# Other TensorE durations in a planned instruction order: a hybrid decoder trunk in float32 on one core

## The chip, the cores and the metric

The kernel runs on one core of a Trainium2 chip. The metric is device time in microseconds (us). Five engines work side by side, each through its own list of instructions, in order: TensorE (PE, with its weight loads as PEld), VectorE (DVE), ScalarE (ACT), GpSimd (POOL) and SyncE (SP), which issues the transfers from memory. The program's order is fixed when it is built; at run time each engine only waits for the semaphores of what it needs.

## The reference, cut to what matters

A trunk of two layers over one sequence of 256 positions of width 1024. Each layer is a feed-forward block (half weight), a token mixer, and a second feed-forward block; every block is normalised and modulated by vectors made of a conditioning vector `c`.

```python
def modulate(x, g, shift, scale):
    return rmsnorm(x, g) * (1.0 + scale[:, None, :]) + shift[:, None, :]

def swiglu(h, w_gu, w_down):                  # w_gu 1024 x 5632, w_down 2816 x 1024
    g, u = jnp.split(h @ w_gu, 2, axis=-1)
    return (jax.nn.silu(g) * u) @ w_down

c_act = jax.nn.silu(c)
for l in range(2):
    mod = (c_act @ w_mod[l] + b_mod[l]).reshape(1, 9, 1024)      # w_mod[l] 1024 x 9216
    h = modulate(x, g_norm[l, 0], mod[:, 0], mod[:, 1])
    x = x + 0.5 * mod[:, 2][:, None, :] * swiglu(h, w_ffn1_gu[l], w_ffn1_down[l])
    h = modulate(x, g_norm[l, 1], mod[:, 3], mod[:, 4])
    x = x + mod[:, 5][:, None, :] * hybrid_mixer(h, ...)         # w_in 1024 x 2048, w_out 1024 x 1024
    h = modulate(x, g_norm[l, 2], mod[:, 6], mod[:, 7])
    x = x + 0.5 * mod[:, 8][:, None, :] * swiglu(h, w_ffn2_gu[l], w_ffn2_down[l])
return rmsnorm(x, g_final)
```

The mixer projects `h` once, runs windowed attention, a gated linear recurrence and a short convolution on parts of the result, and sends all three through one output projection.

## The kernel before

**Products.** Float32 accuracy comes from splitting each operand into a high and a low part. A weight block of 1024 rows and 128 columns is loaded (`raw`), ACT casts its high part (`wH`, line 336) and DVE subtracts to get the low part (`wL`, line 341). The activations are split in the same way into `zH` (line 413) and `zL` (line 416). A product then takes three matmuls of 256 or 258 columns (`mm3`, lines 348 to 350: high by high, high by low, low by high), in the down projection two, one of 256 and one of 512 columns (`mm2`, lines 355 and 356).

**Stages.** Each feed-forward block has 22 output pairs of gate and up columns (`pair`, 8 steps of two products), an evacuation (line 473), a gated activation into `hp`, and then 8 output columns of the down projection with 22 products each, whose sums are added to the residual `xT` (line 491). In the last block before a new stage the next `zH` and `zL` are made right behind each such addition. The mixer does its projections as pairs, its elementwise parts on DVE and ACT, and 64 products of the output projection. The very first block is special (`first`): the modulation of its first eight 128-wide slices is computed on PE (line 975), reduced on DVE (line 979), folded on PE (line 984), turned into scale and shift (lines 987 to 989), and applied (lines 998 to 1003) slice pair by slice pair, while 12 products per slice run in k order.

**Modulation.** The other 16 vectors of `mod` are computed on DVE: each takes 8 transfers of 512 KB (`mraw`, line 368) and 8 passes (lines 373 and 375), one reduction (line 379), a small product on PE and an addition (line 387). One such transfer with its pass is called a *piece* below. They depend on nothing but `c`, so they can stand anywhere before their use; only three `mraw` buffers exist.

**What sets the order.** Every step is put into a list with an engine, an assumed duration, and what it reads and writes (`add`). `due` walks this list backwards and gives each step a latest start, counted from where PE would be if its assumed durations simply followed each other. `emit` then plays the list forward: at each moment it takes the engine that can start earliest, and on it the step with the earliest latest start among those that can start within 0.06 us. Buffers are limited (three `raw`, three `mraw`, eight pairs of `wH` and `wL`, three PSUM tiles for products). The steps are written out in the order of these planned starts. So the assumed durations decide which step an engine's list has first; at run time they have no effect of their own.

The assumed durations of PE's products are the constants `C3` and `C3U` at line 358: `2 * C3U` for a step of a pair (line 482), `2 * C3` for two products of the first block (line 537), `C3` for a product of the down projection (line 568) and of the mixer's output projection (line 844).

## Time and profile before

| | us |
|---|---|
| median of 3 runs | 978.92 |
| lowest and highest | 978.75 and 979.3 |
| the profiled execution, device time | 978.36 |
| its span, first to last instruction | 976.6 |
| PE busy in the span | 957.1 |
| DVE busy | 798.2 |
| ACT busy | 503.1 |
| mean TensorE clock granted, share of full speed | 0.996 |

The profiled execution took 978.36 us, 0.56 us under the median, and its span is 1.76 us shorter than its device time. The views used further down are the page's busy times, busy times by stretches of the span, the waits of an engine summed by what it waited for, and the instructions of one engine in order of time. A square bracket at a row's end gives the idle time of the engine just before it and what ended it. Matmuls overlap, so the pitch from one start to the next, not the printed length, is what a matmul costs PE.

### The profile page before, as it was taken

The numbers are of one execution on the slowest core, as the hardware profiler recorded it, in microseconds if no ns is written. First come the engines' busy times: TensorE is split into PE (matmuls) and PEld (weight loads), VectorE is DVE, ScalarE is ACT, GpSimd is POOL, SyncE is SP. The second block draws the span as 40 slices with busy tenths as digits, with TensorE's granted clock in tenths as the row PEclk, the third lists the DMA queues.
The fourth block names the chain that finished last, engine by engine and source line by source line (L and its number), as shares of the span: only waits on it lengthen the run. The fifth ranks groups of instructions, "written<-read, shape, count | busy, mean of one in ns | idle before, by whom it ended". The sixth has DMA issues, their size and how long they took to land.

```text
span 976.6 us, 18186 instructions
## 1 busy us (share of the span) xinstructions
PE 957.1 (98%) x7407; PEld 905.9 (93%) x7407; DVE 798.2 (82%) x1195; ACT 503.1 (52%) x780; POOL 21.7 (2%) x24
## 2 busy tenths in 40 slices
PE   7999999999999999999999999999999999999997
PEld 6889999889998999998899999988998999999886
DVE  5588989999989999989789976687999998766651
ACT  3446645454865554444454544444577555544431
POOL 5000000000000000000000000000000000000000
PEclk9999999999999999999999999999999999999998
DMA  9976889998946989997878965598785776756421
GB/s 331 367 243 222 272 283 301 364 307 292 246 161 228 301 275 327 311 308 253 294 230 295 312 199 184 190 311 264 253 232 173 249 251 212 243 179 194 163 76 44
DMA packets 185784, 242.76 MB, mean 249 GB/s; under 512 B 6504, under 2 KB 164452, under 8 KB 185700
## 3 DMA queue, kind: packets, MB, share of 16 engines
q1 hardware_dynamic: 185160, 240.96, 75.5%
q8 instruction: 58, 0.95, 0.4%
q10 hardware_dynamic: 540, 0.63, 0.2%
q14 instruction: 26, 0.21, 0.1%
HBM read 240.52 MB, written 1.05 MB: 247 GB/s over the span
## 4 chain that ended last, share of the span: by engine, by line
PE 91%; DVE 3%; DMA 3%; issue 1%; ACT 1%; ACTq 0%; POOLq 0%; DVEq 0%; SPq 0%
PE gu L348 22%; PE gu L349 22%; PE gu L350 22%; PE gu L356 15%; PE gu L355 8%; DMA hp_t<-in_w_mod_dram 1%; DVE wL L341 1%; DMA mraw_t<-in_w_mod_dram 1%; DMA sq_t<-in_b_mod_dram 1%; DVE xT L491 1%; PE gu L632 1%; PE gu L693 1%; DVE macc_t L375 1%; PE s L712 0%; PE s L752 0%
## 5 line engine op out<-in xcount | busy, mean ns | idle before, releaser
L348 PE MATMUL gu<-zH,wH 128*128 128x258 f32 (+1 forms) x1664 | 472.5, 284 | 2.5 <-ACT zH L1002 2.5
L349 PE MATMUL gu<-zL,wH 128*128 128x258 f32 (+1 forms) x1664 | 469.8, 282 | 1.1 <-DVE zL L416 0.3
L350 PE MATMUL gu<-zH,wL 128*128 128x258 f32 (+1 forms) x1664 | 470.7, 283 | 0.0
L336 ACT CAST wH<-raw_t 128x1024 fp32r<-128x1024 f32 (+1 forms) x324 | 320.2, 1015 | 283.8 <-PE gu L356 116.3
L341 DVE TENSOR_TENSOR wL<-raw_t,wH 128x1024 fp32r<-128x1024 f32 (+1 forms) x324 | 375.7, 1181 | 62.8 <-ACT wH L336 61.4
L348 PEld LDWEIGHTS gu<-zH,wH 128*128 128x128 f32 x1664 | 315.3, 189 | 4.8 <-ACT zH L1002 3.9
L349 PEld LDWEIGHTS gu<-zL,wH 128*128 128x128 f32 x1664 | 315.5, 190 | 3.1 <-DVE zL L416 1.9
L350 PEld LDWEIGHTS gu<-zH,wL 128*128 128x128 f32 x1664 | 314.4, 189 | 0.0
L356 PE MATMUL gu<-hp_t,wH 128*128 128x512 f32 x704 | 247.9, 393 | 0.0
L355 PE MATMUL gu<-hp_t,wL 128*128 128x256 f32 x704 | 200.4, 285 | 1.2 <-DVE xT L491 1.2
L356 PEld LDWEIGHTS gu<-hp_t,wH 128*128 128x128 f32 x704 | 132.2, 188 | 29.6
L375 DVE SCALAR_TENSOR_TENSOR macc_t<-mraw_t,cact,macc_t 128x1024 f32<-128x1024 f32 x112 | 143.4, 1280 | 5.6 <-DMA mraw_t<-in_w_mod_dram 5.5
L355 PEld LDWEIGHTS gu<-hp_t,wL 128*128 128x128 f32 x704 | 132.3, 188 | 1.9 <-PE gu L1100 1.1
L473 DVE TENSOR_TENSOR ev_t<-gu,Rb 128x514 f32<-128x514 f32 x98 | 67.5, 690 | 47.4 <-PE gu L350 46.8
L517 ACT CAST hp_t<-h_t 128x256 fp32r<-128x256 f32 x88 | 35.6, 404 | 75.1 <-DVE h_t L515 74.9
L513 ACT ACTIVATE sg_t<-ev_t 128x256 f32<-128x256 f32 x88 | 44.1, 502 | 38.7 <-DVE ev_t L473 35.9
L491 DVE SCALAR_TENSOR_TENSOR xT<-gu,gv_t,xT 128x256 f32<-128x256 f32 x80 | 36.7, 479 | 16.7 <-PE gu L356 16.0
L518 DVE TENSOR_TENSOR hp_t<-h_t,hp_t 128x256 fp32r<-128x256 f32 x88 | 36.9, 420 | 9.0 <-ACT hp_t L517 8.8
L515 DVE SCALAR_TENSOR_TENSOR h_t<-ev_t,sg_t 128x256 f32<-128x256 f32 x88 | 41.7, 475 | 0.5 <-ACT sg_t L513 0.2
L349 PE MATMUL gu<-hp_t,wH 128*128 128x256 f32 x128 | 36.2, 283 | 1.8 <-DVE hp_t L832 1.8
L348 PE MATMUL gu<-hp_t,wH 128*128 128x256 f32 x128 | 37.2, 290 | 0.0
L350 PE MATMUL gu<-hp_t,wL 128*128 128x256 f32 x128 | 36.1, 282 | 0.0
(167 smaller groups left out, 498.2 us busy)
## 6 DMA issues: line engine op xcount, KB each, us to landing
raw_t<-in_w_ffn_gu_dram SPq DMA_DIRECT2D x82, 1024.0 KB, 6.8
mraw_t<-in_w_mod_dram SPq DMA_DIRECT2D x128, 512.0 KB, 6.8
raw_t<-in_w_ffn_down_dram SPq DMA_DIRECT2D x32, 1024.0 KB, 5.4
raw_t<-in_w_ffn_down_dram SPq DMA_DIRECT2D x16, 768.0 KB, 6.7
raw_t<-in_w_in_dram SPq DMA_DIRECT2D x12, 1024.0 KB, 6.4
hp_t<-in_w_mod_dram SPq DMA_DIRECT2D x8, 1024.0 KB, 11.2
raw_t<-in_w_ffn_gu_dram SPq DMA_DIRECT2D x16, 384.0 KB, 8.2
raw_t<-in_w_in_dram SPq DMA_DIRECT2D x8, 512.0 KB, 5.0
```

The costliest lines, as they stand in the source:

```text
L336: A.copy(dst(0), view(raw()))
L341: V.tensor_tensor(out=dst(1), in0=view(raw()), in1=h, op=ALU.subtract)
L348: PE.matmul(ps, lhsT=wh[:, wi, :], rhs=aH, start=first, stop=False, skip_group_check=True)
L349: PE.matmul(ps, lhsT=wh[:, wi, :], rhs=aL, start=False, stop=False, skip_group_check=True)
L350: PE.matmul(ps, lhsT=wl[:, wi, :], rhs=aH, start=False, stop=last, skip_group_check=True)
L355: PE.matmul(ps[:, 0:S], lhsT=wl[:, wi, :], rhs=a[:, 0, :], start=first, stop=False, skip_group_check=True)
L356: PE.matmul(ps, lhsT=wh[:, wi, :], rhs=a, start=False, stop=last, skip_group_check=True)
L375: V.scalar_tensor_tensor(out=acc(), in0=raw(), scalar=cact[:, k:k + 1], in1=acc(), op0=ALU.mult, op1=ALU.add)
L473: V.tensor_tensor(out=t()[:, :, 0:257], in0=ps()[:, :, 0:257], in1=Rb[:, R, 0:257].unsqueeze(1).to_broadcast([128, 2, 257]), op=ALU.mult)
L491: add("DVE", 0.4, lambda: V.scalar_tensor_tensor(out=xT[:, d, :], in0=src(), scalar=gv()[:, d:d + 1], in1=xT[:, d, :], op0=ALU.mult, op1=A ...
L513: add("ACT", ca(S, 1), lambda: A.activation(out=sg(), in_=t()[:, 0, 0:S], func=ACTF.Silu, bias=bg_()), r=[t], w=[sg])
L515: add("DVE", 0.4, lambda: V.scalar_tensor_tensor(out=h(), in0=t()[:, 1, 0:S], scalar=bu_(), in1=sg(), op0=ALU.add, op1=ALU.mult), r=[t, sg ...
```

## The change

One more constant, and three other values: a product in three matmuls of 256 columns is now assumed at 0.357 us instead of 0.3256, in three of 258 columns at 0.3588 instead of 0.3302, and the down projection's product in two matmuls gets a constant of its own, 0.352 instead of 0.3256.

```diff
-    C3, C3U = 0.3256, 0.3302
+    C2, C3, C3U = 0.352, 0.357, 0.3588
...
-                        add("PE", C3, go, r=[(w, 0), (w, 1), (hp, 0, ff % 4), (hp, 1, ff % 4)], w=[ps])
+                        add("PE", C2, go, r=[(w, 0), (w, 1), (hp, 0, ff % 4), (hp, 1, ff % 4)], w=[ps])
```

No instruction is added, removed or altered; only the order on each engine differs. Three places show how.

**The first block.** PE, where the last fold of the modulation (line 984) and the spreading of the norm (line 460) stand. Before, 72 matmuls of two slices stand between the last line 975 and this fold:

```order
L349 MATMUL gu<-zL,wH 128x256
L350 MATMUL gu<-zH,wL 128x256
L984 MATMUL s<-t_t,fold 32x4 x4
L460 MATMUL s<-sq_t,ones 128x256
L348 MATMUL gu<-zH,wH 128x256
```

Now:

```order
L350 MATMUL gu<-zH,wL 128x256
L984 MATMUL s<-t_t,fold 32x4 x4
L975 MATMUL s<-hp_t,c_75 32x256 x16
L984 MATMUL s<-t_t,fold 32x4 x4
L460 MATMUL s<-sq_t,ones 128x256
L348 MATMUL gu<-zH,wH 128x256
```

The last fold follows directly on the last line 975, and the products of the last four slices stand behind it in one piece of 144 matmuls.

DVE at the same place, from the scale and shift of the third slice pair on. Before:

```order
L989 TENSOR_TENSOR a_t<-s,bT 128x2
L1000 SCALAR_TENSOR_TENSOR h_t<-ssum_t,a_t,sg_t 128x256 x2
L1003 TENSOR_TENSOR zL<-h_t,zH 128x256
L979 TENSOR_REDUCE t_t<-s 128x16
L1003 TENSOR_TENSOR zL<-h_t,zH 128x256
L341 TENSOR_TENSOR wL<-raw_t,wH 128x768 x4
L341 TENSOR_TENSOR wL<-raw_t,wH 128x1024
L373 TENSOR_SCALAR macc_t<-mraw_t,cact 128x1024
L375 SCALAR_TENSOR_TENSOR macc_t<-mraw_t,cact,macc_t 128x1024
L987 TENSOR_TENSOR a_t<-s,pt 128x2
```

Now:

```order
L989 TENSOR_TENSOR a_t<-s,bT 128x2
L341 TENSOR_TENSOR wL<-raw_t,wH 128x768
L1000 SCALAR_TENSOR_TENSOR h_t<-ssum_t,a_t,sg_t 128x256 x2
L979 TENSOR_REDUCE t_t<-s 128x16
L1003 TENSOR_TENSOR zL<-h_t,zH 128x256
L341 TENSOR_TENSOR wL<-raw_t,wH 128x768
L1003 TENSOR_TENSOR zL<-h_t,zH 128x256
L987 TENSOR_TENSOR a_t<-s,pt 128x2
```

One `wL` has moved ahead of line 1000, the reduction of line 979 ahead of the first line 1003, and line 987 of the last slice pair ahead of three weight blocks and two passes of a modulation vector. On ACT the cast of the same weight block stands ahead of line 998 now.

**The first block's transfers.** SP, around the first transfer of its down weights. Before:

```order
L368 DMA mraw_t<-in_w_mod_dram 128x1024 x2
L272 DMA raw_t<-in_w_ffn_gu_dram 128x8x256
L272 DMA raw_t<-in_w_ffn_down_dram 128x8x256
L368 DMA mraw_t<-in_w_mod_dram 128x1024 x2
L272 DMA raw_t<-in_w_ffn_down_dram 128x8x256
L272 DMA raw_t<-in_w_ffn_down_dram 128x6x256
L272 DMA raw_t<-in_w_ffn_down_dram 128x8x256
L368 DMA mraw_t<-in_w_mod_dram 128x1024
```

Now:

```order
L368 DMA mraw_t<-in_w_mod_dram 128x1024 x3
L272 DMA raw_t<-in_w_ffn_gu_dram 128x8x256
L272 DMA raw_t<-in_w_ffn_down_dram 128x8x256
L368 DMA mraw_t<-in_w_mod_dram 128x1024 x3
L272 DMA raw_t<-in_w_ffn_down_dram 128x8x256
L272 DMA raw_t<-in_w_ffn_down_dram 128x6x256
L368 DMA mraw_t<-in_w_mod_dram 128x1024
L272 DMA raw_t<-in_w_ffn_down_dram 128x8x256
```

More modulation transfers stand between the same weights: 15 instead of 13 pieces are ahead of the first down transfer, and 35 instead of 27 ahead of the mixer's first one. On DVE 26 instead of 20 passes stand ahead of the block's first line 491 and 35 instead of 31 ahead of its last; ahead of the first line 491 of the mixer it is 51 instead of 48.

**The end of the first mixer.** DVE, from the evacuation of the mixer's last pair (line 473) to the low part of the output projection's last operand (line 832). Before:

```order
L473 TENSOR_TENSOR ev_t<-gu,Rb 128x2x257
L375 SCALAR_TENSOR_TENSOR macc_t<-mraw_t,cact,macc_t 128x1024
L341 TENSOR_TENSOR wL<-raw_t,wH 128x1024
L375 SCALAR_TENSOR_TENSOR macc_t<-mraw_t,cact,macc_t 128x1024
L724 TENSOR_TENSOR hp_t<-s,hp_t 128x4x128
L375 SCALAR_TENSOR_TENSOR macc_t<-mraw_t,cact,macc_t 128x1024
L724 TENSOR_TENSOR hp_t<-s,hp_t 128x4x128
L341 TENSOR_TENSOR wL<-raw_t,wH 128x1024
```

and, after three more pairs of lines 375 and 341 and a reduction, lines 728 and 832. Now:

```order
L473 TENSOR_TENSOR ev_t<-gu,Rb 128x2x257
L375 SCALAR_TENSOR_TENSOR macc_t<-mraw_t,cact,macc_t 128x1024
L341 TENSOR_TENSOR wL<-raw_t,wH 128x1024
L375 SCALAR_TENSOR_TENSOR macc_t<-mraw_t,cact,macc_t 128x1024
L724 TENSOR_TENSOR hp_t<-s,hp_t 128x4x128
L728 SCALAR_TENSOR_TENSOR big_t<-big_t,pt 128x255 x2
L728 SCALAR_TENSOR_TENSOR big_t<-big_t,pt 128x254 x2
L728 SCALAR_TENSOR_TENSOR big_t<-ev_t,big_t 128x256 x2
L341 TENSOR_TENSOR wL<-raw_t,wH 128x1024 x2
L832 TENSOR_TENSOR hp_t<-big_t,hp_t 128x512
```

Two passes instead of six, no reduction and three `wL` instead of six stand between the two.

Behind line 832, up to the residual additions (line 491), DVE had before:

```order
L832 TENSOR_TENSOR hp_t<-big_t,hp_t 128x512
L863 COPY gv_t<-mod 128x8
L397 SCALAR_TENSOR_TENSOR a_t<-mod,pt 128x8
L341 TENSOR_TENSOR wL<-raw_t,wH 128x1024 x2
L404 CAST zH<-mod 128x8
L341 TENSOR_TENSOR wL<-raw_t,wH 128x1024
L491 SCALAR_TENSOR_TENSOR xT<-gu,gv_t,xT 128x256 x3
```

Now line 832 is followed by three `wL`, the reduction of line 379, three small steps of line 387 with one more `wL` between them, and these, the first row being the last of the three:

```order
L387 TENSOR_TENSOR mod<-s,bT 128x8
L397 SCALAR_TENSOR_TENSOR a_t<-mod,pt 128x8
L404 CAST zH<-mod 128x8
L373 TENSOR_SCALAR macc_t<-mraw_t,cact 128x1024
L407 TENSOR_TENSOR zL<-mod,zH 128x8
L375 SCALAR_TENSOR_TENSOR macc_t<-mraw_t,cact,macc_t 128x1024
L341 TENSOR_TENSOR wL<-raw_t,wH 128x1024
L375 SCALAR_TENSOR_TENSOR macc_t<-mraw_t,cact,macc_t 128x1024
L341 TENSOR_TENSOR wL<-raw_t,wH 128x1024
L491 SCALAR_TENSOR_TENSOR xT<-gu,gv_t,xT 128x256 x3
```

So six `wL`, three passes and a reduction stand between line 832 and the additions, where three `wL` stood before. The second mixer shows the same pattern; the gate and up part of the second layer's last block and all behind it stand nearly as before.

## Rows read from the trace of the kernel before

**Rows 1.** By stretches: start:end, length, PE PEld DVE ACT POOL busy, clock, DMA share, GB/s.

```profile
0.00:25.00 25.00, 18.99 (x176) 15.74 (x177) 13.46 (x37) 9.43 (x16) 13.85 (x18) 1.00 0.98 333
25.00:50.00 25.00, 24.28 (x244) 21.62 (x244) 14.65 (x27) 11.84 (x20) 0.00 (x0) 1.00 1.07 368
50.00:75.00 25.00, 22.98 (x179) 22.04 (x179) 19.69 (x30) 9.64 (x17) 0.00 (x0) 0.93 0.73 244
75.00:100.00 25.00, 25.00 (x211) 25.00 (x211) 21.46 (x60) 16.43 (x25) 0.00 (x0) 1.00 0.69 223
75.00:230.00 155.00, 155.00 (x1148) 146.69 (x1148) 142.26 (x217) 81.88 (x116) 0.00 (x0) 1.00 0.89 292
230.00:302.00 72.00, 72.00 (x603) 67.57 (x602) 66.88 (x119) 46.37 (x92) 0.70 (x1) 1.00 0.78 235
```

**Rows 2.** PE in order of time around the first block's last folds: start, length, instruction.

```profile
45.05 1.91 PE L975 MATMUL s<-hp_t,c 128*32 128x256 f32 x32
...
56.35 0.24 PE L984 MATMUL s<-t_t,fold 128*32 128x4 f32 x8
56.53 0.70 PE L460 MATMUL s<-sq_t,ones 128*128 128x256 f32 x2
59.17 0.38 PE L348 MATMUL gu<-zH,wH 128*128 128x256 f32 x1 [1.94 <-ACT zH L1002]
...
69.78 0.26 PE L1019 MATMUL s<-ident,ssum_t 44*128 44x44 f32 x1
```

**Rows 3.** DVE, and last ACT, in order of time at the same place.

```profile
45.55 0.15 DVE L989 TENSOR_TENSOR a_t<-s,bT 128x2 f32<-128x2 f32 x1
46.27 0.89 DVE L1000 SCALAR_TENSOR_TENSOR h_t<-ssum_t,a_t,sg_t 128x256 f32<-128x256 f32 x2 [0.57 <-ACT sg_t L998]
...
47.57 0.71 DVE L979 TRANSPOSE_TENSOR_REDUCE t_t<-s 128x16 f32<-128x512 f32 x1
...
48.62 3.56 DVE L341 TENSOR_TENSOR wL<-raw_t,wH 128x768 fp32r<-128x768 f32 x4
...
45.73 0.91 ACT L998 ACTIVATE sg_t<-xT,a_t 128x256 f32<-128x256 f32 x2 [6.61 <-DVE a_t L989]
```

**Rows 4.** DVE's waits from 225 to 318 us: total, times, longest.

```profile
DVE ev_t L473 <- PE gu L350: 2.1, 3, 1.1
DVE sm_t L672 <- ACT sm_t L669: 1.5, 1, 1.5
DVE macc_t L375 <- DMA mraw_t<-in_w_mod_dram: 1.1, 1, 1.1
```

**Rows 5.** DVE in order of time at the first mixer's end.

```profile
287.17 1.28 DVE L375 SCALAR_TENSOR_TENSOR macc_t<-mraw_t,cact,macc_t 128x1024 f32<-128x1024 f32 x1
288.36 0.69 DVE L724 TENSOR_TENSOR hp_t<-s,hp_t 128x512 fp32r<-128x512 f32 x1
...
301.14 2.35 DVE L341 TENSOR_TENSOR wL<-raw_t,wH 128x1024 fp32r<-128x1024 f32 x2
303.41 0.68 DVE L832 TENSOR_TENSOR hp_t<-big_t,hp_t 128x512 fp32r<-128x512 f32 x1
...
307.64 1.26 DVE L491 SCALAR_TENSOR_TENSOR xT<-gu,gv_t,xT 128x256 f32<-128x256 f32 x3
```

**Rows 6.** PE in order of time at the same place.

```profile
304.15 0.39 PE L349 MATMUL gu<-hp_t,wH 128*128 128x256 f32 x1 [1.84 <-DVE hp_t L832]
...
311.26 0.28 PE L348 MATMUL gu<-zH,wH 128*128 128x258 f32 x1
311.68 0.38 PE L349 MATMUL gu<-zL,wH 128*128 128x258 f32 x1
```

**Rows 7.** PE in order of time in the second layer, two short waits.

```profile
663.52 0.36 PE L355 MATMUL gu<-hp_t,wL 128*128 128x256 f32 x1 [0.29 <-DVE xT L491]
...
775.64 0.39 PE L349 MATMUL gu<-zL,wH 128*128 128x258 f32 x1 [0.31 <-DVE zL L416]
```

**Rows 8.** ACT's waits in the whole span, the largest.

```profile
ACT wH L336 <- PE gu L356: 116.3, 79, 3.0
```

## The prediction, as it went on record

> **What bounds the kernel now.** I read first the busy times by stretches [rows 1]. From 75 us on PE is busy without a gap: 211 matmuls in 25.00 us, a pitch of 0.1185 us, or 0.3555 us for a product in three. So the order of the other engines can only matter where PE stands still, and all that can be gained is the sum of those places. I then looked for them in PE's instructions in order of time. There are four. At the start PE waits 1.94 us for `zH` of slice 6 behind the last fold, and from 50 to 75 us the mean clock is 0.93 [rows 1, 2]: 7% of 25 us at the lower of the two levels, 1.2 GHz, is 3.5 us at half speed, so about 1.7 us are lost; the fall came right behind that wait. At the end of the first mixer PE waits 1.84 us for line 832, and then runs behind DVE: four steps of the next pair show 0.42 us from line 348 to line 349 (311.26 to 311.68) where 0.12 is normal, 4 x 0.30 = 1.2 us [rows 6]. In the second layer there are two waits of 0.3 us [rows 7]. Later, the additions of the last down projection and the tail cost some time, but the order there hardly differs.
>
> The second view is DVE's. It has 142.26 of 155 us busy from 75 to 230 us, and 66.88 of 72 up to 302 [rows 1]; that is 12.7 and 5.1 us idle. In the mixer it waits three times for PE's pairs (2.1 us), once for ACT (1.5) and once for a modulation transfer (1.1) [rows 4], and still brings line 832 too late. So DVE is late there because of what stands in its list, not for want of time over the whole block. The third view, ACT's waits, shows the reserve: ACT stands 116.3 us before its casts because PE has not freed a weight buffer [rows 8], so in steady stretches all eight `wH`, `wL` pairs are full.
>
> **The start.** The order on PE puts the last fold (line 984) and line 460 directly behind the last line 975 instead of 24 products later. I follow the new order from the scale and shift of slices 4 and 5, finished at 45.55 + 0.15 = 45.7 [rows 3]. DVE: one `wL` of 768 columns, 3.56 / 4 = 0.89, to 46.6; line 1000 twice, 0.8 from start to start, to 47.4; line 979, 0.71, to 48.1; then `zL`. PE has ended line 975 at 45.05 + 1.91 = 46.96 [rows 2], waits for line 979, folds at about 48.3 and, with 56.35 to 57.23 = 0.88 us for fold and line 460, begins the products at 49.2. Behind that stand 144 matmuls in one piece, 144 x 0.1185 = 17.1, to 66.3. Line 1019, which follows them, began at 69.78 [rows 2]. **Gain 3.5 us.** The scale and shift of the last slices then have 49.2 + 2 x 4.3 = 57.8 us as their due time and are made by about 53; that cover is 4 us thick. The `wH` cast that now stands ahead of line 998 on ACT needs its weights by 44.7: the loads up to them are 14.9 MB (the input 1.0, eight modulation blocks of 1.05, seven weight slices of 0.79), of which 8.3 came in the first 25 us at 333 GB/s, and the rest takes 18 us at 368 GB/s [rows 1], so they land at about 43, and ACT idled 6.61 us there [rows 3]. If they were late, each us would cost one. If the clock falls behind the new, shorter stand of some 1.3 us too, 1.7 us of the gain go: the two waits before 25 us were followed by no fall (clock 1.00 [rows 1]), so I give that 1 in 4.
>
> **The first block's transfers and passes.** Eight more pieces of 0.524 MB are asked for before the mixer's first weights. From 75 to 230 us the transfers moved 292 GB/s x 155 us = 45.3 MB at a share of 0.89 [rows 1], 328 GB/s while busy; 4.2 MB more take 12.8 us, and 0.11 x 155 = 17 us are free. DVE gets four more passes before the block's end, 4 x 1.19 (287.17 to 288.36 [rows 5]) = 4.8 us, against 12.7 us idle. So both fit, the transfers with 4 us to spare, and I take zero. The bounds: nothing, or a wait of up to the 12.8 us less the reserve of eight weight buffers; six full ones beside the pair in use are three pairs, 3 x 16 x 0.3555 = 17 us of PE's work, so a wait from this alone is unlikely. SP also issues the small constant loads two pieces sooner; nothing on PE reads them before the mixer, and the two pieces are not due before the down products, so this costs nothing. The Trainium skill, "DMA: Bandwidth & Descriptors" (Specifications), gives a limit of about 358 GB/s for one core's share of the memory. By that figure the 49.5 MB would take 138 us of 155 and the spare would be 17 us; the row's 328 makes it 4, and 368 in one stretch is above the page's limit, so the measurement decides.
>
> **The end of the mixer.** Ahead of line 832 stand as many passes as before (48), but the reduction and three small steps have gone behind it: 1.4 us less work. Four of the passes lie before the mixer now, so within the mixer DVE has 6.2 us less to do before line 832. If the first block takes up its 4.8 us, line 832 ends at 304.1 - 6.2 = 297.9, against 302.3 at which PE stood ready (304.15 - 1.84): the wait of 1.84 us goes, with 4 us to spare. What is late next is the addition of line 491. Counted from the start, three passes (3.1 us, the first is shorter) and three `wL` (3 x 1.135 = 3.4, from 301.14 to 303.41 [rows 5]) more stand ahead of it: at 307.64 + 6.5 less what idle time takes up. PE could have its first sums ready at 302.3 + 8 x 0.3555 = 305.1. So 6.5 us taken up bring the addition level with before, 9.0 give the whole gain. The first block has room for its 4.8; within the mixer the waits for pairs, for ACT and for the transfer hold 4.7 [rows 4], and the new order puts work ahead of each: passes and a reduction before the evacuations, a `wL` and other steps before line 672, and the passes at 291 us draw on transfers asked for earlier. 4.8 + 4.7 = 9.5, just over 9.0. **Gain 2.9 us**, of 1.84 + 1.2 = 3.0; bounds 3.0 and a loss of 6.5.
>
> **The second layer.** The x additions at 663 us change places with a `wL` (0.29), the second mixer gets the first one's pattern (0.31) [rows 7]. **Gain 0.5 us**; bounds 0.6 and, by the reckoning of the first mixer with nothing taken up, a loss of 6.2.
>
> **Sum.** 3.5 + 2.9 + 0.5 = 6.9 us off the profiled execution's 978.36 is 971.5; it lies 0.56 below the median of 978.92, so the median becomes 972.0.
>
> **The rivals.**
> *The backlog is not taken up* (slower). The extra passes sit in one list with the weights' low parts, and their transfers in one queue. If DVE's idle time stays as it is, because the passes wait for their transfers, the additions at the mixer's end come 6.5 us later than before, every `zL` with them, and PE waits in the open: with the start's 3.5 us passed through, 978.9 - 3.5 + 6.5 - 0.5 is 981.4; with the start's gain swallowed as well (PE arrives earlier and only waits longer) 985. It decides at 2.5 us taken up (6.5 less 3.5 and 0.5): below that the whole is slower. Against it: 17 us of free transfer time and 17.8 of DVE. For it: three `mraw` buffers, each of which makes DVE stand when a transfer is late (1.1 us at 291). 8 in 100.
> *The waits only move.* The start's gain is kept or the mixer's, not both, because PE arriving 3.5 us earlier meets DVE or the transfers as late as before: 974.5 to 976.9. 14 in 100. If both are lost, or the clock falls as well, it is within 0.2%: 977 to 980.9. 10 in 100.
> *More than the sum.* The new values are near the pitch (0.3588 against 0.3555), so the order may fit better in places where waits are too short to be seen in the rows: 968 to 969.5, 8 in 100.
> *The change does nothing.* If DVE's list had been right by luck, the new one would be no better; but the wait for line 832 stands behind passes that nobody needs before line 397, which speaks against it. It is in the 10 above.
>
> **How the numbers follow.** The forecast, 969.5 to 974.5, has 60 in 100. The range from 968.0 to 977.5 takes in the second and the last rival and leaves out most of the 18 of no change and slower. A measurement of this kernel can tell about 0.2%, 2 us, from no change. Faster by more than that: 60 + 14 + 8 = 82; within: 10; slower: 8.
>
> **What the profile after would show.** PE's first line 1019 near 66 us instead of 69.78, a stand of about 1.3 us at 47 and none at 57, a clock of 1.00 from 50 to 75. PE without a wait for line 832, and steps of 0.12 us in the pair behind the mixer. DVE busier from 75 to 230 than 142 of 155, and without the waits of rows 4. I am wrong if PE waits between 100 and 230 us, if the fold's wait is longer than 2 us, or if line 491 of the mixer ends more than 9 us behind line 832 with PE waiting.

## The result and the profile after

The changed kernel takes 991.14 us (median of 4 runs, 989.42 to 995.09) beside 978.84 us of the kernel before on the same chip: a ratio of 1.0131, 95% interval 1.0112 to 1.015. It is 12.3 us **slower** where I forecast 6.9 us faster. The profiled execution took 995.09 us, the slowest of the four.

The page of after (busy times; and the chain that ended last, by engine):

```profile
PE 962.5 (97%) x7407; PEld 911.7 (92%) x7407; DVE 797.1 (80%) x1195; ACT 504.6 (51%) x780; POOL 22.7 (2%) x24
PE 66%; DVE 14%; DMA 11%; ACT 5%; issue 4%; SPq 1%; POOL 0%; ACTq 0%; DVEq 0%; POOLq 0%
```

The work is the same. The chain that ended last, though, now runs for a quarter of the span through DVE and transfers (14% and 11%; in the kernel before 3% and 3%). Where PE stood, by what it waited for (us in total, times, longest):

```profile
PE gu L348 <- DVE ev_t L505: 5.6, 1, 5.6
PE gu L355 <- DVE xT L491: 5.4, 3, 2.3
PE s L384 <- DVE mod L387: 3.9, 2, 2.2
PE gu L348 <- DVE ev_t L473: 2.2, 2, 1.9
PE gu L348 <- ACT zH L1002: 0.3, 1, 0.3
```

The first, third and fourth of these were not there before, and the second came to 1.2 us; gone are the wait of 1.94 us for `zH` ([rows 2]) and that for line 832 ([rows 6]). Set side by side at equal work done by PE, the changed kernel's profile lies 5 us behind the one before from 75 to 175 us of the latter, 10 us at 230, 12 us from 330 to 650 and 17 us from 785 us on. After in stretches, as [rows 1] (us; busy PE, PEld, DVE, ACT, POOL; granted clock, DMA share, GB/s):

```profile
50.00:57.00 7.00, 7.00 (x61) 7.00 (x61) 6.93 (x14) 3.55 (x7) 0.00 (x0) 1.00 1.05 369
57.00:67.00 10.00, 10.00 (x86) 9.86 (x85) 5.00 (x6) 4.00 (x4) 0.00 (x0) 1.00 0.30 82
67.00:73.00 6.00, 0.39 (x2) 0.30 (x3) 2.85 (x4) 0.68 (x2) 0.00 (x0) 0.87 0.95 334
73.00:78.00 5.00, 5.00 (x24) 5.00 (x25) 4.86 (x10) 3.87 (x8) 0.00 (x0) 0.50 1.10 356
175.00:200.00 25.00, 22.78 (x137) 19.57 (x136) 21.81 (x26) 9.21 (x11) 0.00 (x0) 1.00 0.97 325
310.00:317.00 7.00, 6.50 (x43) 6.22 (x44) 6.11 (x13) 1.05 (x1) 0.00 (x0) 0.52 0.99 324
```

There are three places in the first half, and the second mixer repeats the third.

**At 67 us.** PE's list at the fold, and at line 1019:

```profile
49.12 0.25 PE L984 MATMUL s<-t_t,fold 128*32 128x4 f32 x8 [1.08 <-DVE t_t L979]
66.92 0.26 PE L1019 MATMUL s<-ident,ssum_t 44*128 44x44 f32 x1
72.79 0.55 PE L348 MATMUL gu<-zH,wH 128*128 128x258 f32 x1 [5.61 <-DVE ev_t L505]
```

The start did what I wrote: a short stand at the fold, none at 57 us, line 1019 at 66.92 instead of 69.78. It would have come earlier still: in this execution the clock was at the lower level for 3.4 us from 23.6 us on, where the kernel before kept 1.00 [rows 1] with the same order up to there. Half of that, 1.7 us, is not to be put down to the change. Then PE stood 5.6 us for line 505, and ran the next 5 us at the lower clock. DVE meanwhile:

```profile
70.15 1.29 DVE L375 SCALAR_TENSOR_TENSOR macc_t<-mraw_t,cact,macc_t 128x1024 f32<-128x1024 f32 x1 [7.46 <-DMA mraw_t<-in_w_mod_dram]
71.36 1.28 DVE L505 TENSOR_TENSOR ev_t<-gu,Rb 128x512 f32<-128x512 f32 x2
```

DVE was idle for 7.46 us ahead of line 505, because the fourth pass stands first in its list and its piece had not come. SP's queue says why (the last column of names is what is loaded):

```profile
53.92 0.79 SPq L881 DMA_DIRECT2D ssum_t<-in_lru_conv_w_dram  x1
...
60.86 1.35 SPq L1032 DMA_DIRECT2D gatew<-in_lru_gate_a_w_dram  x2
...
66.22 1.48 SPq L368 DMA_DIRECT2D mraw_t<-in_w_mod_dram  x3
```

From 53.9 to 66.1 us SP issues nothing but small loads (4.0 of these 12.2 us it waits; 82 GB/s from 57 to 67 us), and the fourth piece is issued behind them. Before, two pieces more stood ahead of them, the small loads lasted from 56.43 to 68.45 us, and the fourth pass ran at 63.91 us.

**At 185 and 203 us.** DVE ahead of the first addition of the first down projection:

```profile
183.90 1.28 DVE L375 SCALAR_TENSOR_TENSOR macc_t<-mraw_t,cact,macc_t 128x1024 f32<-128x1024 f32 x1 [1.47 <-DMA mraw_t<-in_w_mod_dram]
185.10 0.95 DVE L341 TENSOR_TENSOR wL<-raw_t,wH 128x768 fp32r<-128x768 f32 x1
185.97 0.48 DVE L491 SCALAR_TENSOR_TENSOR xT<-gu,gv_t,xT 128x256 f32<-128x256 f32 x1
```

Again a pass that waits for its piece stands ahead of a step that PE waits for; ahead of the additions at 203 us another one waits 2.4 us. The number of passes from the start to this addition, before (up to 176.6 us) and then after (up to 185.9 us):

```profile
L375 DVE SCALAR_TENSOR_TENSOR macc_t<-mraw_t,cact,macc_t 128x1024 f32<-128x1024 f32 x17 | 21.8, 1280 | 0.0
L373 DVE TENSOR_SCALAR macc_t<-mraw_t,cact 128x1024 f32<-128x1024 f32 x3 | 2.2, 748 | 0.0
```
```profile
L375 DVE SCALAR_TENSOR_TENSOR macc_t<-mraw_t,cact,macc_t 128x1024 f32<-128x1024 f32 x22 | 28.2, 1281 | 9.5 <-DMA mraw_t<-in_w_mod_dram 9.5
L373 DVE TENSOR_SCALAR macc_t<-mraw_t,cact 128x1024 f32<-128x1024 f32 x4 | 3.0, 747 | 0.0
```

20 before and 26 now.

**In the mixers.** PE and DVE at the end of the first one:

```profile
310.50 0.30 PE L384 MATMUL s<-t_t,fold 128*32 128x8 f32 x8 [2.20 <-DVE mod L387]
```
```profile
309.21 1.24 DVE L379 TRANSPOSE_TENSOR_REDUCE t_t<-macc_t 128x32 f32<-128x1024 f32 x1
```

The wait for line 832 has gone, as I wrote; but PE's own list has the fold of a modulation vector (line 384) in its way, which needs the reduction that ends at 310.45 us (the profile puts the wait to line 387, right behind it in DVE's list). No pass waits for its piece there: the reduction comes late behind line 832 and three `wL`. The clock stood at 0.52 from 310 to 317 us. In the second mixer the same fold costs 1.7 us, an evacuation (line 473) 1.9 us.

### The profile page after: what moved, and what is told of

Its sections match the earlier page's. It is cut to its first block, busy times and chain, and to the rows that moved or that the text cites. A ratio compares the mean times of both kernels' runs of the same rounds, so it can differ in the third digit from the quotient of the medians.

```text
span 993.3 us, 18192 instructions
## 1 busy us (share of the span) xinstructions
PE 962.5 (97%) x7407; PEld 911.7 (92%) x7407; DVE 797.1 (80%) x1195; ACT 504.6 (51%) x780; POOL 22.7 (2%) x24
## 4 chain that ended last, share of the span: by engine, by line
PE 66%; DVE 14%; DMA 11%; ACT 5%; issue 4%; SPq 1%; POOL 0%; ACTq 0%; DVEq 0%; POOLq 0%
PE gu L348 15%; PE gu L350 14%; PE gu L349 14%; PE gu L356 14%; PE gu L355 7%; DVE wL L341 5%; DMA mraw_t<-in_w_mod_dram 4%; DMA raw_t<-in_w_ffn_gu_dram 4%; DVE macc_t L375 3%; ACT big_t L659 1%; DMA hp_t<-in_w_mod_dram 1%; DVE ev_t L473 1%; ACT wH L336 1%; DMA sq_t<-in_b_mod_dram 1%; DVE xT L491 1%
## 5 line engine op out<-in xcount | busy, mean ns | idle before, releaser
L348 PE MATMUL gu<-hp_t,wH 128*128 128x256 f32 x128 | 39.1, 305 | 0.0
L349 PE MATMUL gu<-hp_t,wH 128*128 128x256 f32 x128 | 37.8, 295 | 0.0
```

The costliest lines, as they stand in the source:

```text
L348: PE.matmul(ps, lhsT=wh[:, wi, :], rhs=aH, start=first, stop=False, skip_group_check=True)
L349: PE.matmul(ps, lhsT=wh[:, wi, :], rhs=aL, start=False, stop=False, skip_group_check=True)
```

## The experiments

All times are medians; the ratio is to the kernel before on the same chips.

| run | what is new | us | ratio, 95% |
|---|---|---|---|
| only_c2 | C2 alone | 973.7 | 0.9951 (0.9936 to 0.9965) |
| only_c3 | C3 alone | 981.95 | 1.0036 (1.0023 to 1.005) |
| only_c3u | C3U alone | 983.46 | 1.005 (1.0035 to 1.0065) |
| after_small_price | all three, small loads priced | 984.52 | 1.0066 (1.0049 to 1.0083) |
| c2_c3_small | C2, C3, small loads priced | 972.38 | 0.9942 (0.9924 to 0.9961) |
| after_small_330 | all, small loads, rate 330 | 982.18 | 1.0043 (1.0028 to 1.0057) |
| fold_later | the same, fold 3 us later | 980.63 | 1.003 (1.0014 to 1.0046) |
| all_priced | the same, rate 330 only behind 50 us | 983.64 | 1.0051 (1.0029 to 1.0072) |
| half_pieces | small loads priced, pieces halved | 974.78 | 0.996 (0.9943 to 0.9976) |
| half_passes | small loads priced, passes halved | 976.91 | 0.9977 (0.9961 to 0.9992) |
| pieces_on_pool | all three, pieces issued by POOL | 1002.33 | 1.0238 (1.02 to 1.0276) |
| before_pieces_on_pool | none, pieces issued by POOL | 984.9 | 1.0063 (1.0044 to 1.0082) |
| passes_back_block | small loads, passes of the first block put back | 981.78 | 1.0047 (1.0032 to 1.0062) |
| passes_back_all | small loads, all passes put back | 978.85 | 1.0005 (0.9992 to 1.0018) |
| dve_dearer | small loads, DVE 8.7% dearer | 979.55 | 1.0005 (0.9993 to 1.0018) |
| dve_dearer_330 | the same, rate 330 behind 50 us | 979.81 | 1.001 (1.0 to 1.002) |

### Which of the three durations

My theory after the result, **P**: the loss comes wherever a pass stands in DVE's list ahead of a step that PE waits for and its piece is late. Rivals: all three values cost alike (**U**), or the clock is what costs (**K**).

```diff
-    C2, C3, C3U = 0.352, 0.357, 0.3588
+    C2, C3, C3U = 0.3256, 0.357, 0.3302      # only_c3
+    C2, C3, C3U = 0.3256, 0.3256, 0.3588     # only_c3u
+    C2, C3, C3U = 0.352, 0.3256, 0.3302      # only_c2
```

> Of the three durations only that of the first three chunks and of the mixer's output products (C3) is new, 0.357; the other two are as before. Theory P (a pass that stands in DVE's list ahead of a step that PE waits for, and whose piece is issued too late, makes the loss): the plan still puts the fold of the last slice early and leaves only three of the four pieces ahead of the small loads in SP's queue, so PE's first line 1019 comes near 66 to 67 us, then PE stands 5 to 6 us for line 505 and the clock falls; net from 47 us on 2.8 us later than before, so 981 to 983, and no wait for line 491 between 175 and 215 us. Theory U (all three values work alike, each costs a share of the 12 us): 983, with waits for line 491 too. Theory K (what costs is the clock that falls, not the stand): the same time, but PE would have the same stand without it.

> Only the duration of the pairs' products (C3U) is new, 0.3588. Theory P: the start is that of before (the fold late, five pieces ahead of the small loads), no stand of 5 us behind line 1019; but 24 to 30 passes stand ahead of the first additions of the first down projection (20 to 24 before), so PE waits for line 491 between 175 and 215 us, 4 to 5 us in all, and in the mixers once or twice 2 us for a fold; 983 to 987. Theory U: 983 with a part of the stand at 67 us.

> Only the duration that the diff gives to the down projections' products (C2) is new, 0.352. Theory P: start and first block's passes are those of before, up to two passes more ahead of the last additions; 978 to 980, no new stand above 1 us. Theory U: 983. If neither, and the time is above 985, the down products are what the change costs.

A wait of PE in only_c3, and then three in only_c3u:

```profile
PE gu L348 <- DVE ev_t L505: 6.1, 1, 6.1
```
```profile
PE gu L355 <- DVE xT L491: 4.5, 2, 3.6
PE gu L348 <- DVE ev_t L473: 3.0, 3, 2.0
PE gu L348 <- ACT zH L1002: 2.5, 3, 1.9
```

C3 alone makes the stand at 67 us, and C3U alone those of the first down projection and of the mixer's evacuations, with the start left as it was. Both times lie within P's numbers. Two things do not fit P, though. C3 alone also makes a stand of 1.6 us at the first mixer's fold; and in only_c3u no pass waits for its piece in the 9 us of DVE's list ahead of the longest stand (3.6 us, ended at 183.5 us), so it is the length of the list there, not a late piece. C2 surprised me: alone it gains 4.85 us, where P had expected nothing. PE's stretch through the first mixer in that run, and line 832 on DVE:

```profile
230.00:302.00 72.00, 72.00 (x605) 67.67 (x604) 68.06 (x123) 48.51 (x95) 1.73 (x1) 1.00 0.73 231
298.58 0.69 DVE L832 TENSOR_TENSOR hp_t<-big_t,hp_t 128x512 fp32r<-128x512 f32 x1
```

Line 832 starts 4.8 us earlier than in [rows 5], and PE does not wait for it: it is the gain that the prediction had forecast for the end of the mixer. Three more passes stand ahead of the block's last addition (34 for 31), and four instead of six between the mixer's last evacuation and line 832. The three parts sum to +3.5 us, and the whole change is +12.3: they are not independent. U falls, since each value moves the time in its own way. K can be a part at most: in only_c3 the stand alone is 6.1 us, and half of the 6.8 us at the lower clock that came with it is 3.4.

### The start: the price of the small loads

```diff
-        add(eng, dur, lambda: e.dma_start(...), ...)
+        add(eng, 0.35 if eng == "SP" and kb == 8 else dur, lambda: e.dma_start(...), ...)
...
-        add("SP", 0.6, f1, r=["gates0", ("zL", 7)], w=["gates"], base=base, kb=131.0)
+        add("SP", 5.1, f1, r=["gates0", ("zL", 7)], w=["gates"], base=base, kb=131.0)
```

> The changed kernel, but the plan prices SP's small loads at what the trace shows: 0.35 us instead of 0.1 for each of the seven tables, 5.1 instead of 0.6 for the eight gate loads. The fourth pass then goes behind the evacuations of line 505 in DVE's list; the rest of the order stays nearly that of the changed kernel. Theory P: PE's stand of 5.9 us behind line 1019 goes, and with it the fall of the clock (6.8 us at half speed, 3.4 us): 8 to 9 us below the changed kernel, 982 to 983.5; the waits of 2 to 2.7 us at 185, 203, 308 and 778 us stay. Rival (DVE is late there for want of time, or the gates' loads themselves hold the transfers): 0 to 3 us below, 988 to 991.

PE at the same place in that run, and DVE and PE in two later stretches (columns as above):

```profile
65.29 0.26 PE L1019 MATMUL s<-ident,ssum_t 44*128 44x44 f32 x1
65.48 0.39 PE L348 MATMUL gu<-zH,wH 128*128 128x258 f32 x1
```
```profile
100.00:175.00 75.00, 75.00 (x589) 72.70 (x588) 73.29 (x91) 36.25 (x53) 0.00 (x0) 1.00 0.94 326
175.00:183.00 8.00, 3.54 (x15) 2.83 (x15) 7.96 (x11) 3.56 (x5) 0.00 (x0) 0.86 1.02 361
```

The stand and the low clock behind it have gone, and line 1019 comes 4.5 us earlier than before the change. The whole gained 6.6 us rather than 8 to 9. Part of it came back at 176 us, where PE, now early, stood 4.5 us instead of 2.2. DVE was busy 7.96 of the 8 us there: no piece is late at that place, there is too much ahead of the additions in DVE's list. That is not what P says.

Then the same prices without the new C3U:

> C2 and C3 new (0.352, 0.357), C3U as before (0.3302), and the small loads priced at 0.35 and 5.1 us. The plan sets the fold of the last slice early, three passes ahead of line 505, and 20 to 31 passes ahead of the additions of the first down projection (20 to 28 before, 26 to 32 in the changed kernel). Theory P: the start's gain of 4.2 us (as in the run with the small price) and the gain of the run with C2 alone (4.85 us) add up: 968.5 to 971, no stand at 67 us, none above 1 us between 175 and 215 us. Rival (the gains don't add, since PE that comes 4 us earlier meets DVE and the transfers as late as before): 973 to 979, with a stand in the first down projection.

972.38: from 60 us on PE has no stand above 0.9 us, and this order is **faster than both kernels**, by 6.0 us against the one before on the same chip (978.35). It is 1.4 to 3.9 us over what I expected; its clock fell at 23.2 us for 3.4 us (half of that is lost), at the place, and in the order, of the fall in the changed kernel's profile. DVE had 71.38 of 75 us busy from 100 to 175 us here.

So what remains to be explained is C3U's 12.1 us between 972.38 and 984.52.

### What C3U costs: transfers, DVE's time or the queue

**T**: transfers are late that the plan takes as landed. **D**: DVE has too much in its list. **Q**: pieces and weights hold each other up in SP's queue. half_pieces leaves out half of each piece's bytes, with passes of the same length; half_passes leaves out half of the columns of all passes but a vector's first.

```diff
-                wire = max(wire, o.end + 1.9) + o.kb / 360.0
+                wire = max(wire, o.end + 1.9) + o.kb / 330.0       # after_small_330
...
-   nc.sync.dma_start(out=raw(), in_=w_mod[..., v * D:v * D + D])
+   nc.sync.dma_start(out=raw()[:, 0:512], in_=w_mod[..., v * D:v * D + 512])   # half_pieces
+   nc.gpsimd.dma_start(out=raw(), in_=w_mod[..., v * D:v * D + D])             # pieces_on_pool
...
-   V.scalar_tensor_tensor(out=acc(), in0=raw(), ..., in1=acc(), ...)
+   V.scalar_tensor_tensor(out=acc()[:, 0:512], in0=raw()[:, 0:512], ..., in1=acc()[:, 0:512], ...)   # half_passes
```

> The changed kernel with the small loads priced as in the run before, and the plan's rate of transfers 330 instead of 360 KB per us (the traces show 325 to 341 GB/s while the queue is full). The fold of the last slice goes back behind the products, as before the change; 24 to 29 passes stand ahead of the first additions of the first down projection (26 to 31 without). Theory T (passes and weights wait there for transfers that the plan takes as landed): the stand of 4.9 us at 176 us goes or falls below 1.5 us; without the start's gain 979 to 982. Rival D (DVE has too much in its list there whatever the transfers): the stand stays near 4 to 5 us, 986 to 989, since the start's gain is lost.

> The order of the run with the small price, but each piece of the modulation weights is loaded only in its first half (0.262 MB instead of 0.524), and the pass reads that half twice, so that DVE's work has the same length; the modulation is another one. Theory T (late transfers): PE's stand of 4.9 us at 176 us goes, and DVE's waits for wH between 60 and 230 us (11.3 us) shrink to less than half; 976 to 979. Rival D (too much work in DVE's list): the stand stays above 3 us; 982 to 986.

> The order of the run with the small price and the whole transfers, but each pass behind the first of a vector works on 512 of the 1024 columns (0.6 us less each); the rest of the sum is left out. Theory T: DVE still waits for the casts, which wait for the transfers; the stand at 176 us shrinks by the 0.6 us of each pass behind the last wait (three to five: 2 to 3 us) and stays above 1.5 us. Rival D: the stand goes altogether, and those at 269, 302 and 767 us as well (1.9, 1.6 and 1.9 us with the fall of the clock): 974 to 977.

With 330 the stand at 176 us went altogether (T), but the start's gain was lost as expected, and two folds took the stand's place. PE's wait and DVE ahead of the first:

```profile
PE s L384 <- DVE mod L387: 5.1, 2, 3.1
```
```profile
298.28 1.23 DVE L341 TENSOR_TENSOR wL<-raw_t,wH 128x1024 fp32r<-128x1024 f32 x1 [3.02 <-ACT wH L336]
299.42 1.24 DVE L379 TRANSPOSE_TENSOR_REDUCE t_t<-macc_t 128x32 f32<-128x1024 f32 x1
```

The two halves split it. The stretch from 100 to 175 us of half_pieces, and then of half_passes:

```profile
100.00:175.00 75.00, 75.00 (x588) 72.65 (x588) 73.91 (x91) 37.93 (x53) 0.00 (x0) 1.00 0.82 269
```
```profile
100.00:175.00 75.00, 75.00 (x588) 72.69 (x588) 65.52 (x92) 36.44 (x52) 0.00 (x0) 1.00 0.95 328
```

Half the bytes left DVE at 73.91 of 75 us, and the stand at 176 us shrank from 4.5 to 2.0 us. Half the work left the transfers at 0.95, DVE waited 19.4 us for casts from 60 to 230 us (11.3 in after_small_price), and the stand shrank to 2.2. For half_passes that is the stand that T foretold, with the time of D; for half_pieces it is neither's. So neither came out alone: DVE and the transfers are both full there.

> The changed kernel with its order, but the pieces of the modulation weights are issued by POOL instead of SP, so that nothing in SP's queue (small loads, weights) stands ahead of a piece or behind one. Theory Q (the order in the one queue makes pieces and weights late): the stand of 5.9 us at 67 us falls below 1.5 us, and those at 185, 203, 308 and 778 us below 1 us; 974 to 979. Theory T (the transfers as a whole are too slow there for so many pieces): the stand at 67 goes, the others stay; 982 to 986. If POOL's own steps (the powers of line 437) come late behind a piece that waits for a buffer, PE stands behind lines 460 and 473 in new places; 985 to 995.

> The kernel before with its order, the pieces issued by POOL. A control for the run above: by theory Q nothing is behind a piece in the kernel before that PE waits for but line 832 at the end of the first mixer: 976 to 979. Above 980: issuing by POOL costs by itself.

PE of pieces_on_pool at line 1019, and three of its waits:

```profile
72.02 0.26 PE L1019 MATMUL s<-ident,ssum_t 44*128 44x44 f32 x1
72.20 0.39 PE L348 MATMUL gu<-zH,wH 128*128 128x258 f32 x1
```
```profile
PE gu L355 <- DVE xT L491: 5.9, 2, 5.1
PE s L975 <- DMA hp_t<-in_w_mod_dram: 5.6, 1, 5.6
PE s L384 <- DVE mod L387: 3.1, 1, 3.1
```

The stand behind line 1019 went, which shows once more that it was the place in SP's queue. The others did not go (the additions 5.9 us in all, 5.4 in the changed kernel; the folds 3.1 and 3.9), so Q falls for them. But 1002.33 is above all that I had expected. In both runs on POOL the first slices come late: PE waits 5.3 and 5.6 us for line 975 at 21 us, where it waited 1.8 and 1.2. POOL asks for its first three pieces at 14.8 us, beside those slices; not line 437, which I had feared. In the kernel before, the longer wait and 6.8 us at the lower clock behind it account for the 6.4 us that issuing by POOL cost. In the changed kernel the rest stands elsewhere, as in the 5.1 us of line 491 with another 6.8 us at the lower clock.

### The fold, and everything priced

```diff
-                rt[q.idx] = max(rt[q.idx], o.end + lat)
+                rt[q.idx] = max(rt[q.idx], o.end + lat + (FOLD if q.eng == "PE" and q.base == 1e9 and o.dur == 1.14 else 0.0))   # FOLD = 3.0
...
+                wire = max(wire, o.end + 1.9) + o.kb / (360.0 if wire < 50.0 else 330.0)       # all_priced
```

> The order of the changed kernel with small loads priced and the rate at 330, as in that run, and one thing more: in the plan the fold of a modulation vector (line 384) is ready 3 us behind its reduction (line 379) instead of 0.2. In both mixers the fold of the last vector goes from behind 39 to behind 47 of the 64 output products. Theory F (PE stands at the fold because the plan left it no slack behind DVE, and DVE is 3 us behind the plan there): the stands of 3.35 us at 297 and 2.29 us at 765 go, and the fall of the clock behind the first (1.7 us): 974 to 977. Rival (DVE is late with everything by then, so that PE meets the next thing late, line 491 or the zL): 979 to 982, with new stands of 1 to 3 us behind the mixers.

> All three new durations, the small loads priced, the fold 3 us behind its reduction, and the plan's rate of transfers 360 up to the 50th us and 330 behind it, so that the fold of the last slice stays early; 26 and 30 passes stand ahead of the first additions of the first down projection (24 and 29 with 330 throughout). If the first block's stand comes from transfers that the plan takes as landed, it is gone here as well, and the start's gain of 4.2 us comes to the 975 expected with the later fold: 970 to 973. Rival (with PE 4 us earlier the passes and additions are late again): a stand of 2 to 5 us between 174 and 206 us, 974 to 979.

fold_later took the stands at the folds away and gained 1.6 us, not 5 to 8; the intervals of the two ratios overlap. The next thing was late, in the second mixer (DVE and PE):

```profile
770.05 2.61 DVE L375 SCALAR_TENSOR_TENSOR macc_t<-mraw_t,cact,macc_t 128x1024 f32<-128x1024 f32 x2
772.57 1.65 DVE L491 SCALAR_TENSOR_TENSOR xT<-gu,gv_t,xT 128x256 f32<-128x256 f32 x4
```
```profile
773.65 0.39 PE L348 MATMUL gu<-zH,wH 128*128 128x258 f32 x1 [1.44 <-ACT zH L413]
```

Two passes stand ahead of the additions there too. all_priced, with every price put right that I had found wrong, took 983.64 us, above both ranges that I had given and above the kernel before. It kept the early fold and got the stand at 176 us back (3.5 us for line 491, without one wait of a pass for its piece from 60 to 230 us; DVE 74.11 of 75 us busy from 100 to 175). So the rate does not remove that stand by itself. In after_small_330 PE came 4 us later, and 24 passes instead of 26 stood ahead of the first addition; which of the two took the stand away is not shown.

### The passes put back, and DVE dearer

```diff
+        for q, p in PIN.items():          # PIN: pass -> the step of PE behind which it starts with C3U = 0.3302
+            need[q] += 1
+            succ[p].append(self.ops[q])
```

> All three new durations and the small loads priced (984.5 us), but the 5th to the 36th pass may not start in the plan ahead of the step of PE behind which they start with C3U as before (972.4 us); so 20, 26 and 31 passes stand ahead of the additions of the first down projection instead of 26, 31 and 32. Nothing else is changed; the passes in the mixer stay. Theory L (the passes' place in the list is the cause: six more of them, 7 us of DVE and 3.1 MB, ahead of the additions at 176 us): the stand of 4.9 us at 176 us goes, with the fall of the clock behind it (1.7 us), and the stand at 269 us may go with it (1.9): 975 to 978. Rival (the order of PE and of the weights with C3U new is what costs): the stand stays above 2.5 us; 982 to 986.

> As the run before, but all passes from the 5th on, in both layers, go back to the places that they have with C3U as before. Theory L: the stands in the mixers (1.6 us at 302, 1.9 us at 767) go as well; 971.5 to 974, level with 972.4. Rival (what is left in the mixers comes from other things that C3U moves, folds and casts): 975 to 979, with stands at the folds of the mixers of 1.5 us or more.

```diff
-        o = Op()
+        o = Op(); dur *= MORE.get(eng, 1.0)      # MORE = {"DVE": 1.087}
```

> All three new durations, the small loads priced, and every DVE step 8.7% dearer in the plan (0.3588 / 0.3302), nothing else. In the order 20, 24 and 29 passes stand ahead of the additions of the first down projection (26, 31 and 32 without), the fold of the last slice stays early, the fold of the last vector goes to behind 43 of 64 output products in the first mixer and stays behind 37 in the second. Theory M (what C3U takes away is the margin that the plan had for a late DVE; given back on DVE's side, the stands go): no stand above 1.5 us behind 75 us but one at the fold of the second mixer; 970 to 975. Rival (PE stands for casts and weights that the transfers bring late, which a dearer DVE doesn't change): stands of 2 us and more at 176 and 269 us stay; 979 to 984.

> As the run before, and the plan's rate of transfers 330 behind the 50th us: 20, 24 and 28 passes ahead of the additions, the first mixer's fold behind 47. Theory M: like the run before or up to 2 us faster, 969 to 974. Rival of that (the rate makes the plan put off passes that then stand in the mixer): 975 to 980, with stands between 255 and 310 us.

The passes' place is about half of C3U's cost: 5.7 of 12.1 us with all of them put back, 2.7 with those of the first block. Both were less than I had expected of them. With the small loads priced and all passes put back the kernel is level with the one before (978.85, ratio 1.0005): these two steps account for the whole loss. Why the 6 us that c2_c3_small gains are missing there, the other half of C3U's cost, was not taken apart and stays open. In passes_back_all four stands of 0.7 to 1.5 us remained, at an addition, an evacuation and two folds, every one behind DVE. Making DVE dearer by the factor by which C3U had grown took away every stand above 0.3 us behind 75 us but those at the end of the first mixer (and the 0.9 us in the last down projection, there before as well), and gained 5.0 us; I had expected 9 or more, and 979.55 is no better than the kernel before. The longest of those at the mixer's end, in PE's waits of dve_dearer:

```profile
PE s L384 <- DVE t_t L379: 1.8, 1, 1.8
```

So the margin removes the stands of the first block and of the second mixer. At the end of the first mixer it brought back the list of the kernel before: six passes, six `wL` and the reduction stand again between the last evacuation and line 832 (in the changed kernel two, three and none), and the last of the passes waits for its piece:

```profile
294.70 1.29 DVE L375 SCALAR_TENSOR_TENSOR macc_t<-mraw_t,cact,macc_t 128x1024 f32<-128x1024 f32 x1 [2.15 <-DMA mraw_t<-in_w_mod_dram]
```

In dve_dearer_330 it is seven passes, and PE waits 1.8 us for line 832, as in [rows 6]. So the margin undoes at that place what only_c2 had gained.

## Why the prediction was wrong, step by step

**What bounds the kernel.** Right: PE without gaps, and only the places where it stands can be gained. What I did not draw from it is the other side: an order that leaves PE four stands in a whole run has much to lose.

**The start, gain 3.5 us.** The fold's term was right: PE waited 1.08 us there and the clock stayed at 1.00 from 50 to 57 us; line 1019 came 2.9 us earlier in the profiled run, in spite of the 1.7 us lost to the clock at 23.6 us, and 4.5 us in after_small_price. What failed is a sentence of the next part, "SP also issues the small constant loads two pieces sooner; nothing on PE reads them before the mixer, and the two pieces are not due before the down products, so this costs nothing". I asked who reads the small loads, not what is issued behind them, and took the date by which a pass is needed for its place in DVE's list. The fourth pass stands ahead of line 505, and its piece behind the 12.2 us of small loads. only_c3 shows the cost (+3.4 us in all, with the fold's gain inside), after_small_price its removal. The plan prices the eight gate loads at 0.6 us; SP took 5.2.

**The first block, zero.** This is the second step that failed. "Four more passes before the block's end" counts at the wrong place: what PE waits for are the additions of line 491, and ahead of the first stand six more passes (20 and 26 by the rows), 7.1 us of DVE at 1.19 and 3.1 MB. And 12.7 us of idle DVE and 17 us of free transfers are sums over 155 us. In shorter stretches the kernel before shows:

```profile
100.00:175.00 75.00, 75.00 (x600) 73.21 (x600) 69.93 (x88) 39.54 (x56) 0.00 (x0) 1.00 0.87 288
150.00:200.00 50.00, 50.00 (x325) 45.13 (x325) 47.41 (x60) 23.63 (x31) 0.00 (x0) 1.00 0.99 337
200.00:230.00 30.00, 30.00 (x198) 26.56 (x198) 28.17 (x43) 14.57 (x23) 0.00 (x0) 1.00 0.97 306
```

From 150 us on the transfers were full already (0.99 and 0.97); the free time lay ahead of that (a share of 0.69 up to 100 us, [rows 1]), and where PE starts 4 us earlier, as in after_small_price, that much of it goes. From 100 to 175 us DVE had 5.1 us free (69.93 of 75); six passes want 7.1. My own mark, "PE waits between 100 and 230 us", is what came.

**The end of the mixer, gain 2.9 us.** The main part of the mechanism, passes taken ahead of the mixer, was right and is C2's: alone it brings line 832 4.8 us earlier and the run, with both mixers in it, 4.85 us down, more than this term and the next. In the whole change it was used up by what the first block no longer took up, and by the fold of line 384, which I had not followed on PE, though it stands in PE's own list among the output products. The reduction that I counted as work gone from ahead of line 832 is what this fold then had to wait for. Line 832 without a wait, as forecast, was no sign of a gain.

**The second layer, gain 0.5 us.** Wrong with the same step: it took the mixer's pattern, with two stands of 1.9 and 1.7 us and 3.4 us of half clock behind the second: some 5 of the 17 us between the two profiles.

**The rivals.** "The backlog is not taken up" had the sign and, for the block, the mechanism, with passes that wait for their pieces in one list; at 981.4 to 985 it was 6 us too cheap, since the start's stand came on top, and 8 in 100 was too little. I weighed it by the same sums over the whole block that had made the term zero.

**The sum.** c2_c3_small comes to 972.38, beside 972.0 predicted: the forecast fits a plan without the new C3U and with the small loads at their price. That is no merit of the sum, whose terms were made for another order; with only_c2 it shows that the start and the mixer can give gains of the size described.

## What to carry to other kernels

A plan that sets an order is right or wrong in the relations of its prices: two products priced too short (C3 and C3U; their new values are 9 to 10% higher) had acted as a margin for what was priced too cheaply elsewhere, the small loads for one, and putting them right exposed that. Putting more prices right did not settle it: with the small loads, the rate and the fold priced as well the kernel took 983.64 us, with a margin on DVE 979.55, and the best order, 972.38, kept C3U as it was. So try each price by itself and look at the order that it makes. When steps move, count them at the first thing that the bound engine waits for, and read idle time in stretches that end there; and for each queue that a step is moved past, ask what is issued behind it, and where its reader stands.

## What the hardware showed that I had not expected

Small loads hold a queue far longer than their bytes: the eight gate loads of 32 KB took SP 0.63 to 0.68 us each (32 KB at 369 GB/s would be 0.09 us), and with the tables before them and the waits between them the queue brought no weights for 12.2 us; the transfers fell to 82 GB/s (57 to 67 us) from 369.

In the profiled execution of the changed kernel the clock fell to the lower level at three of PE's six long stands: at the 5.6 us at 67 us (for 6.8 us), the 2.2 us at 308 (6.8) and the 1.7 us at 778 (3.4), but not at the 2.2 us at 185, the like one at 203 or the 1.9 us at 746 us. It fell for 3.4 us also behind a wait of 1.2 us for the first slices at 22 us; the kernel before, with the same order up to there, waited 1.8 us at that place and kept its clock. The length of the stand alone does not tell which. For the fold I had asked what a fall would cost; for stands that I did not foresee it came on top.

Three pieces of 0.5 MB asked for by another queue at 14.8 us came together with a wait of PE for the first slices that was 3.5 to 4.4 us longer, in both kernels.
